# A two-layer encoder on one core: feed-forward x at another address, a memset on another engine, sums one slot later, scale rows by transposes

## The chip, the core and the metric

The kernel runs on 1 core of one Trainium2 chip. The metric is the device time of one execution in microseconds. The engines go by these names: PE is TensorE (matrix products), PEld its weight load, DVE VectorE, ACT ScalarE, POOL GpSimd, SP SyncE. ACTq and SPq are the queues from which ACT and SP issue DMAs. Each engine works through its own queue in the order in which the program emitted its instructions; semaphores hold an instruction until what it reads or overwrites is ready.

## What is computed

An encoder of two layers over 256 tokens of width 2048, in 32-bit floating point. Each layer adds a mixer (an mLSTM, a retention and an attention with low-rank projections) and a feed-forward part to x:

```python
for l in range(DEPTH):                                  # DEPTH = 2
    h = _rms(x, g_mix[l])
    x = x + _mixer(h, cos, sin, w_in[l], ...)           # h @ w_in, three groups of heads, y @ w_out
    u = _rms(x, g_ffn[l])
    x = x + jnp.square(jax.nn.relu(u @ w_ff1[l])) @ w_ff2[l]   # 2048 -> 8192 -> 2048
return _rms(x, g_final)
```

`_rms` divides each token by its root mean square and multiplies each column by a gain. The kernel applies the gain when it transposes x, and the division by the token (`rs`, one number for each token) only to the products.

## The kernel before

**Operands.** Every large product is done with its operands split into a high and a low part (float32r, names ending in hi and lo): of the four partial products three are computed. x itself (`xx`, two tiles of 128 tokens) stays in SBUF. Its transposed, scaled and split copy is `xT`: for each of 16 blocks of 128 columns (index k) 256 tokens high and then 256 tokens low, so 512 numbers or 2 KB for each partition and k. `make_xT` (L516) writes it anew before each mixer and each feed-forward part, a quarter (b = 0 to 3) at a time: TensorE transposes, ACT writes the high part, DVE the low one. It starts at byte 37632 of each partition, a multiple of 256.

**The weights** are streamed through the chip once. `Stream` (L230) lets SP fetch chunks of 128 x 1024 (512 KB, `wraw`, four buffers); for each chunk ACT makes `whi` (L308) and DVE `wlo` (L309), four buffers each, prepared up to three chunks ahead of PE. Three kinds of loops use them:

- `nat` and `nat_steps` (L464 to L486): x or y is the stationary operand and 512 columns of weights move past it; three matmuls for each k and token tile.
- `stat` (L488): a 128 x 128 piece of weights is stationary and the 256 tokens move.
- `ff_tile` (L1170), the first product of the feed-forward part (FF1): the piece of `whi` is stationary while high and low x move together, 512 wide, and then the piece of `wlo` while high x moves, 256 wide. The sum is tile `f`. There are 64 tiles f for each layer with 16 such pairs each, 2048 pairs in all.

**The feed-forward part** runs in groups of 8 tiles f. While FF1 works at group gi + 1, the second product (FF2) is done for group gi, half of it by plain `nat_steps` into the tiles `pk`, and half by the seven products of a Strassen scheme (`product`, L1194; tiles `pa`, `pd`, `pe`). So the loop at L1251 has slots i = 0 to 7: FF1 of one tile f, product i (not in the last slot), one chunk of plain FF2. The Strassen scheme needs sums of weights (`su`, `sb`, on DVE, L286 to L292) and sums of activations (`ff_sums`, L1152): for each half of a group four DVE instructions into `fsum`, two on ACT (`shi`) and two on DVE (`slo`). The first half's sums of group gi + 1 are handed out after slot i = 4, six times in each layer.

**The order of the work.** Side work (transposes, evacuations, softmax, sums) is written as generators. `pump` (L451) is called between the matmuls with the time that they are thought to take, and lets at most two side tasks that are due make one step. So the order on every queue is fixed when the program is written out, by the estimates given to `yield` and `pump`; a step more or less in one task shifts its neighbours.

**The mLSTM values.** `ev_mlv` (L848) gets a buffer `mlv` of 4 heads x 2 token tiles x 129 columns, sets the last column of each to one (L852, DVE, 128 x 8), and lets ACT copy the values from PSUM beside it (L854), which has to wait for that memset. Ahead of the memset in DVE's queue are the mLSTM convolutions (L834 to L837).

**The token scale.** `token_scale` (L531) reduces the sums of squares, takes the root (`rsqrt`) and then needs `rs`, which lies across partitions, as a row that is repeated in all partitions. For the feed-forward part it does so with two TensorE transposes and a DVE copy (tile `rsf`). For the mixer, at the start of each layer, it writes `rs` to memory (`rs_rows`, L548) and reads it back into all partitions (`rsb`, L550): two DMAs from ACT's queue. `rsb` is first read at L824.

Of the kernel before, what the change touches and what calls it, by code (L numbers as in the profile page):

```python
# [10 lines left out]
F32 = mybir.dt.float32  # L11
F32R = mybir.dt.float32r
# [6 lines left out]
P = 128  # L19
S = 256  # L20
D = 2048
DEPTH = 2
KT = D // P
# [19 lines left out]
G_MIX, G_FFN, G_ML, G_RET, G_Q, G_KV, W_CONV, B_GATE, PAR_W = 0, 16, 32, 36, 40, 44, 46, 70, 86  # L43
# [277 lines left out]
def encoder_kernel(ctx: ExitStack, tc: tile.TileContext, xin, posin, w, par, const, gfin, out, dump=None):  # L321
    nc = tc.nc
    plan = weight_plan()
    one = ctx.enter_context(tc.tile_pool(name="one", bufs=1))
    wp = ctx.enter_context(tc.tile_pool(name="wp", bufs=4))
    ap = ctx.enter_context(tc.tile_pool(name="ap", bufs=1))
    sp = ctx.enter_context(tc.tile_pool(name="sp", bufs=2))
    pm = ctx.enter_context(tc.tile_pool(name="pm", bufs=4, space=PSUM))
    pside = ctx.enter_context(tc.tile_pool(name="pside", bufs=4, space=PSUM))
    dp = ctx.enter_context(tc.tile_pool(name="dp", bufs=2, space=bass.MemoryType.DRAM))  # L330
    ctx.enter_context(tc.manual_schedule())

    V, A, T = nc.vector, nc.scalar, nc.tensor
# [2 lines left out]

    cst = one.tile([P, C_W], F32, name="cst")
    head = one.tile([P, P + DEPTH * PAR_W], F32, name="head")
    pos = one.tile([P, 2], I32, name="pos")
    ss = one.tile([P, 2, 4], F32, name="ss")  # L340
    rs = one.tile([P, 2], F32, name="rs")

    one.tile([P, 40], F32, name="pad")
    xx = one.tile([P, 2, D], F32, name="xx")
    x = [xx[:, t, :] for t in range(2)]
    xT = one.tile([P, KT, 2, S], F32R, name="xT")
    cosf = one.tile([P, 2, 64], F32, name="cosf")
    sinf = one.tile([P, 2, 64], F32, name="sinf")

# [6 lines left out]
    for i, cw in enumerate((256, 256, 512, 512, 512)):  # L356
        nc.sync.dma_start(out=xx[:, :, c0:c0 + cw],
                          in_=xin[:, c0:c0 + cw].rearrange("(t p) c -> p t c", p=P))
# [14 lines left out]
    def bank(name):  # L373
        return pside.tile([P, 512], F32, name=name, tag="s")

    def sumsq(src, acc, width):
        junk = sp.tile([P, 512], mybir.dt.bfloat16, name="junk", tag="junk", bufs=1)
        A.activation(junk[:, :width], src, AF.Square, accum_out=acc)
# [15 lines left out]
    def split(*items):  # L394

        for hi, lo, src, *g in items:
            A.activation(hi, src, AF.Copy, **({"scale": g[0]} if g else {}))
        for hi, lo, src, *g in items:
            if g:
                V.scalar_tensor_tensor(lo, src, g[0], hi.bitcast(F32), op0=ALU.mult, op1=ALU.subtract)  # L400
            else:
                V.tensor_tensor(lo, src, hi.bitcast(F32), op=ALU.subtract)  # L402

    def tr(dst, src, n=P):
        T.transpose(dst, src, ident[:n, :n])
# [8 lines left out]
    class Task:  # L414
# [24 lines left out]
        def finish(self, n=1 << 30):  # L439
            for d in self.after:  # L440
                d, m = d if isinstance(d, tuple) else (d, 1 << 30)
                d.finish(m)
            while not self.done and self.n < n:
                self.step()

    def add(gen, after=(), delay=0.0):
        t = Task(gen, list(after), delay)
        side.append(t)
        return t
# [53 lines left out]
    xt_task = {}  # L503

    def xboth(k):
        if k // 4 in xt_task:
            xt_task[k // 4].finish(1 + k % 4 // 2)
        return xT[:, k, :, :]

    def xh(k):  # L510
        return xboth(k)[:, 0, :]
# [3 lines left out]

    def make_xT(b, g0, l, wait):  # L516

        for pr in range(2):
            ps = bank("xt")
            for j in range(2):  # L520
                k = 4 * b + 2 * pr + j
                for t in range(2):
                    tr(ps[:, j * S + t * P:j * S + (t + 1) * P], x[t][:, k * P:(k + 1) * P])
            k = 4 * b + 2 * pr
            split(*[(xT[:, k + j, 0, :], xT[:, k + j, 1, :], ps[:, j * S:(j + 1) * S],
                     prm[:, l, g0 + k + j:g0 + k + j + 1]) for j in range(2)])
            yield 0.8 if pr == 0 else wait
        for t in range(2):
            sumsq(x[t][:, b * 512:(b + 1) * 512], ss[:, t, b:b + 1], 512)

    def token_scale(rows_by_pe):  # L531
        tot = sp.tile([P, 2], F32, name="tot", tag="tot")
        V.tensor_reduce(tot, ss, axis=AX.X, op=ALU.add)
        yield from rsqrt(rs, tot, 2, 1.0 / D)
        if rows_by_pe:
            yield 1.0
            rsb = sp.tile([P, 2, P], F32, name="rsf", tag="rsb", bufs=1)
            ps = bank("rsf")
            for t in range(2):
                tr(ps[:, t * P:(t + 1) * P], rs[:, t:t + 1].broadcast_to([P, P]))  # L540
            V.tensor_copy(hflat(rsb), ps[:, :S])
            scale_rows.append(rsb)
            return
        rows = dp.tile([2, P], F32, name="rs_rows")
        rsb = sp.tile([P, 2, P], F32, name="rsb", tag="rsb", bufs=1)
        scale_rows.append(rsb)
        yield 2.4
        nc.scalar.dma_start(out=rows.rearrange("t p -> p t"), in_=rs)  # L548
        yield 8.0
        nc.scalar.dma_start(out=rsb, in_=rows.unsqueeze(0).broadcast_to([P, 2, P]))  # L550

    def new_xT(b, g0, l, rows_by_pe, wait=0.8):

        xt_task[b] = add(make_xT(b, g0, l, wait), [(xt_task[b - 1], 2)] if b else [])
        if b == 3:
            xt_last[:] = [add(token_scale(rows_by_pe), xt_task.values(), 1.2)]

    xt_last = []
    scale_rows = []
# [55 lines left out]
    def hflat(tl):  # L615
        return tl.rearrange("p a b -> p (a b)")

    def layer(l):
        g = prm[:, l, :]
        L = {}  # L620


        def ev_cq(ps):
            L["cq"] = ap.tile([P, 2, 512], F32, name="cq", tag="nat", bufs=2)
            L["sq"] = sp.tile([P, 2, 2], F32, name="sq", tag="sq", bufs=1)
            for t in range(2):
                A.activation(L["cq"][:, t, :], ps[t], AF.Copy, scale=rs[:, t:t + 1])
                sumsq(L["cq"][:, t, :], L["sq"][:, 0, t:t + 1], 512)

        def cq_task():  # L630
            cq = L["cq"]
            L["chi"] = ap.tile([P, 6, S], F32R, name="chi", tag="hhi", bufs=2)
            L["clo"] = ap.tile([P, 6, S], F32R, name="clo", tag="hlo", bufs=2)
# [214 lines left out]
        def ev_mlv(ps):  # L848
            finish(gat)
            v = ap.tile([P, 1088], F32, name="mlv", tag="mlv")[:, :1032].rearrange("p (a b c) -> p a b c", a=2, b=4)  # L850
            L["mlv"] = v
            V.memset(v[:, :, :, 128:129].rearrange("p a b c -> p (a b c)"), 1.0)  # L852
            for t in range(2):
                A.activation(v[:, t, :, 0:128], ps[t].rearrange("p (h c) -> p h c", h=4), AF.Copy,  # L854
                             scale=rs[:, t:t + 1])
# [182 lines left out]
        for h in range(0, 8, 4):  # L1038
            ps = [pm.tile([P, 512], F32, name="pm", tag="m") for _ in range(2)]
# [9 lines left out]
        for h in range(0, 8, 2):  # L1049
            ps = pm.tile([P, 512], F32, name="pm", tag="m")  # L1050
# [16 lines left out]
        for i in range(2):  # L1067
            chunks = take()
            pss = []
            for pr in range(2):  # L1070
                ps = pm.tile([P, 512], F32, name="pm", tag="m")
# [43 lines left out]
        for b in range(2):  # L1115
            nat_steps(take(), pss[b], yh, yl, 0, False, True)
            ev_x(b)(pss[b])
            new_xT(b, G_FFN, l, True)
        for b in range(2, 4):
            nat(take(), yh, yl, ev_x(b))  # L1120
            new_xT(b, G_FFN, l, True)


        hts, qs, fs, evs = {}, {}, {}, {}

        def ff_evac(f, ps):
# [111 lines left out]
        ps = [bank("f") for i in range(2)]  # L1238
# [12 lines left out]
        for gi in range(NGRP - 1):  # L1251
            more = gi + 1 < NGRP - 1
            for i in range(8):
                ff1((gi + 1) * 8 + i)
                if i < 7:
                    product(gi, i)
                if not keep:
                    keep += [[pm.tile([P, 512], F32, name="pk", tag="m") for _ in range(2)] for _ in range(2)]
                nat_steps(take(), keep[i // 4], hk(gi, 0), hk(gi, 1), 0, gi == 0 and i % 4 == 0,
                          i == 7 and not more and l == DEPTH - 1)  # L1260
                if more and i == 4:
                    sums[gi + 1, 0] = add(ff_sums(gi + 1, 0), [evs[(gi + 1) * 8 + 3]])
            if more:
                sums[gi + 1, 1] = add(ff_sums(gi + 1, 1), [evs[(gi + 1) * 8 + 7], sums[gi + 1, 0]])
# [4 lines left out]
        for b in range(4):  # L1269
            if l == DEPTH - 1 and b == 3:  # L1270
                last_block(take(), lh, ll)
                return
            ps = keep[b - 2] if b >= 2 else [bank("pb") for t in range(2)]
            nat_steps(take(), ps, lh, ll, 0, b < 2, True)
            ev_x(b)(ps)
            if l + 1 < DEPTH:
                new_xT(b, G_MIX, l + 1, False)
            else:
                add(final_part(b))

# [64 lines left out]
                nc.sync.dma_start(out=out[tok, b * 512:(b + 1) * 512], in_=xs)  # L1345

    for b in range(4):
        new_xT(b, G_MIX, 0, False, 5.0)
    ws.prep(1)
    xt_task[0].finish(1)  # L1350
    tables = [add(rope_tables(), [xt_task[3]])]
# [31 lines left out]
```

## Time and profile before

| | us |
|---|---|
| median of 3 runs | 2151.51 (2151.40 to 2151.62) |
| the profiled execution's own time | 2152.16 |
| its span in the trace | 2150.3 |

The granted clock of TensorE over that execution was 0.997. A row of the profile's list of groups names line, engine and operation, what is written and read, and the count, then busy time, mean duration in ns, and the idle time of the engine ahead of these instructions with what ended it. In a stretch of the timeline a row has start, duration, engine, line, operation, and in brackets the idle time before it. Matmuls overlap: the next one starts while the one before still drains, so the cost of a matmul is read from one start to the next and not from the duration shown.

### The profile page before, as it was taken

The page shows a single profiled execution, that of the slowest core. Times are in us where ns is not written, and L with a number is a line of the kernel's source. Part 1 is how long each engine was busy: PE and PEld are TensorE (multiplying, and loading weights), DVE is VectorE, ACT ScalarE, POOL GpSimd, SP SyncE. Part 2 cuts the span into 40 slices and gives each one's busy share as a digit, 9 for nine tenths or more (in the row PEclk, how much of TensorE's full clock was granted, in tenths as well). Part 3 has the DMA queues.
Part 4 walks back from the last instruction along what each step waited for, and adds up shares of the span by engine and source line. Part 5 has one row for each costly group of instructions (what it writes and reads, how often), then busy time and mean ns, then how long its engine had stood idle before and what let it go on. Part 6 is the DMA issues. An engine that isn't in the chain of part 4 may idle for free.

```text
span 2150.3 us, 29544 instructions
## 1 busy us (share of the span) xinstructions
PE 2121.0 (99%) x11116; PEld 1811.4 (84%) x11116; DVE 1607.2 (75%) x2371; ACT 1215.0 (57%) x1802; POOL 4.1 (0%) x7
## 2 busy tenths in 40 slices
PE   8999999999999999999999999999999999999998
PEld 7898888888888888888888978888888888888887
DVE  5767575788878888887666675758878888788875
ACT  6645655555655555555556456556555555565554
POOL 0000000000000000000000000000000000000000
PEclk9999999999999999999999999999999999999999
DMA  7544555656566566575575454557566565665664
GB/s 212 186 147 134 170 177 186 199 172 227 162 210 208 165 210 201 166 233 160 181 187 173 131 162 133 184 179 234 156 214 196 169 231 156 212 203 168 211 190 158
DMA packets 111359, 395.22 MB, mean 184 GB/s; under 512 B 12904, under 2 KB 14056, under 8 KB 111088
## 3 DMA queue, kind: packets, MB, share of 16 engines
q1 hardware_dynamic: 109072, 389.90, 56.7%
q10 hardware_dynamic: 2144, 3.43, 0.5%
q8 instruction: 87, 1.43, 0.3%
q14 instruction: 56, 0.46, 0.1%
HBM read 391.17 MB, written 2.12 MB: 183 GB/s over the span
## 4 chain that ended last, share of the span: by engine, by line
PE 80%; DVE 12%; ACT 3%; issue 3%; DMA 1%; ACTq 0%; SPq 0%; DVEq 0%
PE f L408 27%; PE pm L408 26%; PE pk L408 13%; DVE wlo L309 6%; ACT whi L308 2%; PE pb L408 2%; PE pa L1221 2%; PE pa L1223 2%; PE pa L1222 2%; DVE sb L290 1%; DMA wraw<-in_w_dram 1%; DVE su L292 1%; PE sc L408 1%; DVE slo L402 1%; DVE xx L1230 1%
## 5 line engine op out<-in xcount | busy, mean ns | idle before, releaser
L309 DVE TENSOR_TENSOR wlo<-wraw,whi 128x1024 fp32r<-128x1024 f32 (+2 forms) x681 | 825.7, 1216 | 286.8 <-ACT whi L308 284.8
L308 ACT ACTIVATE whi<-wraw 128x1024 fp32r<-128x1024 f32 (+2 forms) x681 | 704.8, 1051 | 207.2 <-PE f L408 86.5
L408 PE MATMUL f<-xT,whi 128*128 128x512 f32 x2048 | 731.9, 398 | 0.0
L408 PE MATMUL f<-xT,wlo 128*128 128x256 f32 x2048 | 554.2, 281 | 0.0
L408 PEld LDWEIGHTS f<-xT,whi 128*128 128x128 f32 x2048 | 384.1, 188 | 86.5
L408 PEld LDWEIGHTS f<-xT,wlo 128*128 128x128 f32 x2048 | 386.5, 189 | 11.6
L408 PE MATMUL pm<-whi,xT 128*128 128x512 f32 (+1 forms) x896 | 289.9, 392 | 6.7 <-ACT whi L308 5.0
L408 PE MATMUL pk<-wlo,hhi 128*128 128x512 f32 x496 | 194.4, 392 | 6.2 <-DVE wlo L309 6.2
L408 PEld LDWEIGHTS pm<-whi,xT 128*128 128x128 f32 x896 | 168.5, 191 | 37.8 <-ACT whi L308 6.1
L408 PE MATMUL pk<-whi,hhi 128*128 128x512 f32 x496 | 193.5, 390 | 0.0
L408 PE MATMUL pk<-whi,hlo 128*128 128x512 f32 x496 | 193.2, 389 | 0.0
L408 PE MATMUL pm<-wlo,xT 128*128 128x512 f32 (+1 forms) x448 | 172.4, 385 | 3.6 <-DVE wlo L309 3.6
L1138 ACT ACTIVATE fr<-f 128x256 f32<-128x256 f32 x128 | 48.2, 376 | 152.5 <-PE f L408 152.5
L308 ACT ACTIVATE whi<-su 128x1024 fp32r<-128x1024 f32 x84 | 87.3, 1054 | 72.1 <-DVE su L288 68.3
L309 DVE TENSOR_TENSOR wlo<-su,whi 128x1024 fp32r<-128x1024 f32 x84 | 100.3, 1219 | 34.1 <-ACT whi L308 34.1
L408 PEld LDWEIGHTS pk<-wlo,hhi 128*128 128x128 f32 x496 | 93.1, 188 | 30.3 <-DVE wlo L309 11.3
L1145 ACT ACTIVATE fq<-fu 128x256 f32<-128x256 f32 x128 | 53.6, 418 | 104.2 <-DVE fu L1143 104.1
L408 PEld LDWEIGHTS pk<-whi,hlo 128*128 128x128 f32 x496 | 93.1, 188 | 19.1
L408 PEld LDWEIGHTS pk<-whi,hhi 128*128 128x128 f32 x496 | 93.1, 188 | 18.8
L1139 DVE TENSOR_TENSOR fr<-f,fr 128x256 f32<-128x256 f32 x128 | 53.8, 421 | 65.2 <-ACT fr L1138 65.1
L408 PEld LDWEIGHTS pm<-wlo,xT 128*128 128x128 f32 x448 | 85.6, 191 | 19.4 <-DVE wlo L309 5.9
L408 PE MATMUL pm<-whi,yhi 128*128 128x512 f32 x256 | 101.5, 397 | 0.0
(295 smaller groups left out, 3066.4 us busy)
## 6 DMA issues: line engine op xcount, KB each, us to landing
wraw<-in_w_dram SPq DMA_DIRECT2D x667, 512.0 KB, 3.8
sb<-in_w_dram SPq DMA_DIRECT2D x56, 512.0 KB, 5.9
wraw<-in_w_dram SPq DMA_DIRECT2D x10, 504.0 KB, 6.9
wt<-mx_rows ACTq DMA_DIRECT2D x8, 256.0 KB, 3.5
out_dram<-xx SPq DMA_DIRECT2D x8, 256.0 KB, 3.1
xx<-in_x_dram SPq DMA_DIRECT2D x3, 512.0 KB, 7.7
gf<-in_gfin_dram ACTq DMA_DIRECT2D x1, 1024.0 KB, 5.5
xx<-in_x_dram SPq DMA_DIRECT2D x2, 256.0 KB, 4.2
```

Source lines behind the costliest of these rows:

```text
L290: V.tensor_tensor(held["b12"][:, h, :], held["b12"][:, h, :], held["b22"][:, h, :], op=ALU.add)
L292: V.tensor_tensor(held["u"][:, h, :], held["u"][:, h, :], last, op=ALU.add)
L308: self.nc.scalar.activation(hi[:, :f], raw, AF.Copy)
L309: self.nc.vector.tensor_tensor(lo[:, :f], raw, hi[:, :f].bitcast(F32), op=ALU.subtract)
L402: V.tensor_tensor(lo, src, hi.bitcast(F32), op=ALU.subtract)
L408: T.matmul(ps, lhsT=lhsT, rhs=rhs, start=start, stop=stop)
L1138: A.activation(r, ps[:, S:], AF.Copy)
L1139: V.tensor_tensor(r, ps[:, :S], r, op=ALU.add)
L1145: A.activation(q, u, AF.Square)
L1221: T.matmul(ps, lhsT=ha, rhs=wh, start=st, stop=False, skip_group_check=True)
L1222: T.matmul(ps, lhsT=ha, rhs=wl, start=False, stop=False, skip_group_check=True)
L1223: T.matmul(ps, lhsT=la, rhs=wh, start=False, stop=kp == 3, skip_group_check=True)
```

## The change

Four edits, made together:

1. **x of the feed-forward part lies 32 bytes on.** `xT` becomes a buffer that is 16 numbers longer, with two views of the same shape: one at offset 0, which the mixer uses, and one at offset 8 numbers (32 bytes), which the feed-forward part uses, for writing and for reading. `xx` and the buffer are allocated ahead of `pos`, `ss` and `rs`, and the pad shrinks from 40 to 24 numbers, so that the mixer's view starts at byte 37376 (again a multiple of 256), the feed-forward's at 37408, and everything from `cosf` on stays at its address.
2. **The ones of `mlv`** are set by GpSimd in place of DVE.
3. **The first half of the sums** of the next group is handed out after slot 5 and not after slot 4.
4. **The mixer's token scale rows** are made as the feed-forward's always were, by two transposes and a DVE copy; the two DMAs through memory go. The tile is named `rsb` in both places.

```diff
-    one.tile([P, 40], F32, name="pad")
-    xx = one.tile([P, 2, D], F32, name="xx")
-    xT = one.tile([P, KT, 2, S], F32R, name="xT")
+    xx = one.tile([P, 2, D], F32, name="xx")
...
+    xbuf = one.tile([P, KT * 2 * S + 16], F32R, name="xT")
+    views = [xbuf[:, o:o + KT * 2 * S].rearrange("p (k a s) -> p k a s", k=KT, a=2) for o in (0, 8)]
+    view = [0]
...
+    one.tile([P, 24], F32, name="pad")
...
     def xboth(k):
...
-        return xT[:, k, :, :]
+        return views[view[0]][:, k, :, :]
...
     def make_xT(b, g0, l, wait):
+        xT = views[1 if g0 == G_FFN else 0]
...
-    def token_scale(rows_by_pe):
+    def token_scale():
         tot = sp.tile([P, 2], F32, name="tot", tag="tot")
         V.tensor_reduce(tot, ss, axis=AX.X, op=ALU.add)
         yield from rsqrt(rs, tot, 2, 1.0 / D)
-        if rows_by_pe:
...
-        rows = dp.tile([2, P], F32, name="rs_rows")
+        yield 1.0
         rsb = sp.tile([P, 2, P], F32, name="rsb", tag="rsb", bufs=1)
+        ps = bank("rsb")
+        for t in range(2):
+            tr(ps[:, t * P:(t + 1) * P], rs[:, t:t + 1].broadcast_to([P, P]))
+        V.tensor_copy(hflat(rsb), ps[:, :S])
         scale_rows.append(rsb)
-        yield 2.4
-        nc.scalar.dma_start(out=rows.rearrange("t p -> p t"), in_=rs)
-        yield 8.0
-        nc.scalar.dma_start(out=rsb, in_=rows.unsqueeze(0).broadcast_to([P, 2, P]))
...
-            V.memset(v[:, :, :, 128:129].rearrange("p a b c -> p (a b c)"), 1.0)
+            nc.gpsimd.memset(v[:, :, :, 128:129].rearrange("p a b c -> p (a b c)"), 1.0)
...
+        view[0] = 1
...
-                if more and i == 4:
+                if more and i == 5:
                     sums[gi + 1, 0] = add(ff_sums(gi + 1, 0), [evs[(gi + 1) * 8 + 3]])
```

Three places of the order show what moves. The first is DVE's queue in the feed-forward part of layer 0, where the first half of a group's sums stands (`fsum`, `slo`; `wlo` are the low parts of chunks of weights, `su` the sum of weights for the Strassen scheme, `fr` a step of the evacuation of a tile f; a number behind a name counts the buffers). Before:

```order
L292 TENSOR_TENSOR su<-su,wraw_5192 128x1024
L309 TENSOR_TENSOR wlo_5307<-wraw_5192,whi_5306 128x1024
L1160 TENSOR_TENSOR fsum<-fq 128x256
L1161 SCALAR_TENSOR_TENSOR fsum<-fq,fsum 128x256
L1163 SCALAR_TENSOR_TENSOR fsum<-fsum,fq 128x256
L1164 TENSOR_TENSOR fsum<-fq 128x256
L292 TENSOR_TENSOR su<-su,wraw_5256 128x1024
L309 TENSOR_TENSOR wlo_5339<-wraw_5256,whi_5338 128x1024
L402 TENSOR_TENSOR slo_5321<-fsum,shi_5320 128x2x256
L402 TENSOR_TENSOR slo_5323<-fsum,shi_5322 128x2x256
L309 TENSOR_TENSOR wlo_5366<-wraw_5273,whi_5365 128x1024
L1139 TENSOR_TENSOR fr<-f,fr 128x256
```

The same sums in the queue of after, where they stand behind other chunks:

```order
L309 TENSOR_TENSOR wlo_5406<-su,whi_5405 128x1024
L1157 TENSOR_TENSOR fsum<-fq 128x256
L1158 SCALAR_TENSOR_TENSOR fsum<-fq,fsum 128x256
L1160 SCALAR_TENSOR_TENSOR fsum<-fsum,fq 128x256
L1161 TENSOR_TENSOR fsum<-fq 128x256
L309 TENSOR_TENSOR wlo_5435<-su,whi_5434 128x1024
L404 TENSOR_TENSOR slo_5418<-fsum,shi_5417 128x2x256
L404 TENSOR_TENSOR slo_5420<-fsum,shi_5419 128x2x256
L309 TENSOR_TENSOR wlo_5459<-wraw_5334,whi_5458 128x1024
L1136 TENSOR_TENSOR fr<-f,fr 128x256
L309 TENSOR_TENSOR wlo_5475<-wraw_5357,whi_5474 128x1024
```

The six instructions move from between the two `su` sums of product 5 to between the two chunks of product 6 (`wlo<-su`), which need no new sum of weights. The two `shi` on ACT move with them.

The second place is ACT's queue in layer 0, behind the first chunks of the mixer (`chi` is the split latent of the attention, `g_eu` and `g_r` are the mLSTM's gates, `krh` the rotary key, and an ACT_TABLE_LOAD fetches the table of another function). Before:

```order
L308 ACTIVATE whi_707<-wraw_590 128x1024
L397 ACTIVATE chi<-ckvt,head 128x256 x2
L308 ACTIVATE whi_735<-wraw_617 128x1024
L762 ACT_TABLE_LOAD
L762 ACTIVATE g_eu<-g_eu 4x512
L308 ACTIVATE whi_771<-wraw_652 128x1024
L767 ACT_TABLE_LOAD
L767 ACTIVATE g_r<-g_eu 4x512
L681 ACTIVATE krh<-krt 128x256
L308 ACTIVATE whi_798<-wraw_678 128x1024
```

And after:

```order
L308 ACTIVATE whi_708<-wraw_591 128x1024
L399 ACTIVATE chi<-ckvt,head 128x256 x2
L758 ACT_TABLE_LOAD
L758 ACTIVATE g_eu<-g_eu 4x512
L308 ACTIVATE whi_737<-wraw_618 128x1024
L763 ACT_TABLE_LOAD
L763 ACTIVATE g_r<-g_eu 4x512
L308 ACTIVATE whi_774<-wraw_653 128x1024
L677 ACTIVATE krh<-krt 128x256
L308 ACTIVATE whi_803<-wraw_679 128x1024
```

The token scale task of layer 0 has fewer steps, so the tasks behind it come due elsewhere: `krh` and the gates have changed places with chunks of weights. From the evacuation of c_q on to the mLSTM's columns, layer 0's order on PE, ACT and DVE is now the one that layer 1 has, before and after alike.

The third is GpSimd's queue behind its start. Before:

```order
L1379 UNCONDITIONAL_BRANCH
L363 MEMSET krl 128x256
L964 MEMSET rq 128x2048 x2
L1379 UNCONDITIONAL_BRANCH
L1379 ISA
```

After:

```order
L1376 UNCONDITIONAL_BRANCH
L365 MEMSET krl 128x256
L848 MEMSET mlv 128x8
L960 MEMSET rq 128x2048
L848 MEMSET mlv 128x8
L960 MEMSET rq 128x2048
L1376 UNCONDITIONAL_BRANCH
```

Each layer's memset of ones stands ahead of that layer's memset of `rq`, and behind nothing else of its layer.

More of the change, by code (lines that the diff above doesn't have):

```diff
@@ L338, in encoder_kernel @@
     head = one.tile([P, P + DEPTH * PAR_W], F32, name="head")
+    xx = one.tile([P, 2, D], F32, name="xx")
+    x = [xx[:, t, :] for t in range(2)]
+    xbuf = one.tile([P, KT * 2 * S + 16], F32R, name="xT")
+    views = [xbuf[:, o:o + KT * 2 * S].rearrange("p (k a s) -> p k a s", k=KT, a=2) for o in (0, 8)]
+    view = [0]
     pos = one.tile([P, 2], I32, name="pos")
@@ L341, in encoder_kernel @@
     rs = one.tile([P, 2], F32, name="rs")
-    one.tile([P, 40], F32, name="pad")
-    xx = one.tile([P, 2, D], F32, name="xx")
-    x = [xx[:, t, :] for t in range(2)]
-    xT = one.tile([P, KT, 2, S], F32R, name="xT")
+    one.tile([P, 24], F32, name="pad")
     cosf = one.tile([P, 2, 64], F32, name="cosf")
@@ L534, in token_scale, with new_xT @@
         yield from rsqrt(rs, tot, 2, 1.0 / D)
-        if rows_by_pe:
[L536 to L543, printed above, removed]
-        rows = dp.tile([2, P], F32, name="rs_rows")
+        yield 1.0
         rsb = sp.tile([P, 2, P], F32, name="rsb", tag="rsb", bufs=1)
+        ps = bank("rsb")
+        for t in range(2):
+            tr(ps[:, t * P:(t + 1) * P], rs[:, t:t + 1].broadcast_to([P, P]))
+        V.tensor_copy(hflat(rsb), ps[:, :S])
         scale_rows.append(rsb)
-        yield 2.4
-        nc.scalar.dma_start(out=rows.rearrange("t p -> p t"), in_=rs)
-        yield 8.0
-        nc.scalar.dma_start(out=rsb, in_=rows.unsqueeze(0).broadcast_to([P, 2, P]))
-    def new_xT(b, g0, l, rows_by_pe, wait=0.8):
+    def new_xT(b, g0, l, wait=0.8):
         xt_task[b] = add(make_xT(b, g0, l, wait), [(xt_task[b - 1], 2)] if b else [])
         if b == 3:
-            xt_last[:] = [add(token_scale(rows_by_pe), xt_task.values(), 1.2)]
+            xt_last[:] = [add(token_scale(), xt_task.values(), 1.2)]
     xt_last = []
@@ L620, in layer @@
         L = {}
+        view[0] = 0
         def ev_cq(ps):
@@ L1117, in layer @@
             ev_x(b)(pss[b])
-            new_xT(b, G_FFN, l, True)
+            new_xT(b, G_FFN, l)
         for b in range(2, 4):
             nat(take(), yh, yl, ev_x(b))
-            new_xT(b, G_FFN, l, True)
+            new_xT(b, G_FFN, l)
+        view[0] = 1
         hts, qs, fs, evs = {}, {}, {}, {}
@@ L1276, in layer @@
             if l + 1 < DEPTH:
-                new_xT(b, G_MIX, l + 1, False)
+                new_xT(b, G_MIX, l + 1)
             else:
@@ L1347, in encoder_kernel @@
     for b in range(4):
-        new_xT(b, G_MIX, 0, False, 5.0)
+        new_xT(b, G_MIX, 0, 5.0)
     ws.prep(1)
```

## Prediction

> **What bounds the kernel now.** I read the page's engine line first, then the chain, then what TensorE waited for.
>
> ```profile
> PE 2121.0 (99%) x11116; PEld 1811.4 (84%) x11116; DVE 1607.2 (75%) x2371; ACT 1215.0 (57%) x1802; POOL 4.1 (0%) x7
> PE 80%; DVE 12%; ACT 3%; issue 3%; DMA 1%; ACTq 0%; SPq 0%; DVEq 0%
> L408 PE MATMUL f<-xT,whi 128*128 128x512 f32 x2048 | 731.9, 398 | 0.0
> ```
>
> PE is busy in all but 29 of 2150 us and carries 80% of the chain. So time can go in two ways: PE stops less, or a matmul takes less. The waits of PE say how much the first holds (total, times, longest):
>
> ```profile
> PE pk L408 <- DVE wlo L309: 6.2, 12, 0.5
> PE pm L408 <- DVE wlo L309: 5.6, 10, 0.9
> PE pm L408 <- ACT whi L308: 5.0, 3, 2.0
> ...
> PE krt L405 <- DVE kr L676: 0.9, 2, 0.5
> ```
>
> Twelve equal stalls are in the feed-forward part, in `pk`; most of the rest are in the mixers. For the second way one needs the time from start to start, since shown durations overlap. From PE's timeline, x stationary with 512 weights moving (nine matmuls between the first two rows), and then weights stationary with 256 of x moving (six):
>
> ```profile
> 1276.75 0.62 PE L408 MATMUL pm<-whi,xT 128*128 128x512 f32 x2
> ...
> 1278.79 0.39 PE L408 MATMUL pm<-whi,xT 128*128 128x512 f32 x1
> ```
>
> ```profile
> 140.40 0.28 PE L408 MATMUL pm<-xT,wlo 128*128 128x256 f32 x1
> ...
> 141.12 0.28 PE L408 MATMUL pm<-xT,wlo 128*128 128x256 f32 x1
> ```
>
> 2.04 / 9 = 226.7 ns and 0.72 / 6 = 120 ns. An FF1 pair (512 and 256) should therefore take 346.7 ns. Two tiles `f` show what it takes; from the first to the second row there are 13 pairs, from the third to the last 14:
>
> ```profile
> 391.22 0.40 PE L408 MATMUL f<-xT,whi 128*128 128x512 f32 x1
> ...
> 395.73 0.39 PE L408 MATMUL f<-xT,whi 128*128 128x512 f32 x1
> ...
> 578.87 0.39 PE L408 MATMUL f<-xT,whi 128*128 128x512 f32 x1
> ...
> 579.56 0.40 PE L408 MATMUL f<-xT,whi 128*128 128x512 f32 x1
> ...
> 579.92 0.40 PE L408 MATMUL f<-xT,whi 128*128 128x512 f32 x1
> ...
> 583.80 0.40 PE L408 MATMUL f<-xT,whi 128*128 128x512 f32 x1
> ```
>
> 4.51 / 13 = 346.9 in the early tile and 4.93 / 14 = 352.1 in the later one, which is like nearly all others; within it, pairs take up to 0.36. Averaged over the trace, with the ends of tiles, I take 352.8: an excess of 6.1 ns x 2048 = 12.5 us, with no wait shown.
>
> **Part 1: x 32 bytes on.** Removed or added: nothing but an address. The views of 2 KB for each k overlap the mixer's only where the mixer has long finished, so no new wait. The excess is found where 512 numbers of x move, and not where x is stationary (226.7) or moves 256 wide (120). The early tile used the same x addresses and ran without it, so it can go away; it is a matter of how the reads fall, to which the address may belong. No row shows an operand of these matmuls off a multiple of 256 bytes, so the price is bounded by rows: at best the 512 matmul falls to 226.7 while the 256 one stays at its present 117 (pairs of 344), -18 us; nothing; at worst all pairs as the slowest, 0.36, +15 us, and for a matmul disturbed twice see the rival. I take the pair of the early tile, 346.7 to 346.9, as the nearest row: **-12.5 us**.
>
> A rule of the Trainium skill, TensorE: Matmul & The Clock Gate, Step-by-step: what each phase is for, speaks against this term: TensorE has two independent read ports into SBUF, so that loading weights takes no bandwidth from the moving operand; by it no address should matter and the term is 0. The trace agrees with it where x is stationary (226.7 with a load behind every matmul), and leaves it open in FF1.
>
> **Part 2: the sums one slot later.** One of the twelve stalls, on PE and on DVE:
>
> ```profile
> 575.31 0.39 PE L408 MATMUL pk<-whi,hhi 128*128 128x512 f32 x1
> 576.22 0.50 PE L408 MATMUL pk<-wlo,hhi 128*128 128x512 f32 x1 [0.52 <-DVE wlo L309]
> 576.56 0.40 PE L408 MATMUL pk<-whi,hlo 128*128 128x512 f32 x1
> ```
>
> ```profile
> 569.89 0.42 DVE L1160 TENSOR_TENSOR fsum<-fq 128x256 f32<-128x256 f32 x1
> ...
> 571.48 1.22 DVE L292 TENSOR_TENSOR su<-su,wraw 128x1024 f32<-128x1024 f32 x1
> ...
> 573.75 1.28 DVE L402 TENSOR_TENSOR slo<-fsum,shi 128x512 fp32r<-128x512 f32 x2
> 574.95 1.22 DVE L309 TENSOR_TENSOR wlo<-wraw,whi 128x1024 fp32r<-128x1024 f32 x1
> ...
> 582.86 1.23 DVE L309 TENSOR_TENSOR wlo<-wraw,whi 128x1024 fp32r<-128x1024 f32 x1 [0.55 <-ACT whi L308]
> ```
>
> Two matmuls took 576.56 - 575.31 = 1.25 us where 2 x 0.227 = 0.45 are due: 0.80 us, which is the idle 0.52 and 0.28 that don't show as idle; I use the idle plus 0.28 for other stalls. DVE has no gap from 569.89 to past the late `wlo` at 574.95: in that stretch lie the sums (569.89 to 571.48 and 573.75 to 574.95, 2.8 us) and a weight sum of 1.2 us. In the next slot, product 6, there is no weight sum, and DVE waits for ACT again at 582.86, 0.55 us. The sums arrive there with 1.2 us more room for each chunk that needs none, and the `wlo` behind them were ready 2 us and more ahead of PE; 2.8 us in four pieces uses that up but for little. On ACT the two `shi` move with them, and it waits between its chunks there, too. All twelve stalls go: 12 x 0.80 = **-9.6 us**. If the cover is short, the same stalls come back in slot 6, smaller or equal: 0 to -9.6, the nearest row is the gap, so the far end.
>
> **Part 3: the ones of `mlv`.**
>
> ```profile
> 204.74 1.27 ACT L854 ACTIVATE mlv<-pm,rs 128x512 f32<-128x512 f32 x2 [7.56 <-DVE mlv L852]
> ```
>
> ```profile
> 207.00 0.50 PE L408 MATMUL pm<-whi,xT 128*128 128x512 f32 x1 [1.46 <-ACT whi L308]
> 208.26 0.50 PE L408 MATMUL pm<-wlo,xT 128*128 128x512 f32 x1 [0.76 <-DVE wlo L309]
> ...
> 211.74 0.50 PE L408 MATMUL pm<-wlo,xT 128*128 128x512 f32 x1 [0.42 <-DVE wlo L309]
> ...
> 1272.55 1.06 PE L408 MATMUL pm<-whi,xT 128*128 128x512 f32 x2
> ...
> 1275.83 0.40 PE L408 MATMUL pm<-wlo,xT 128*128 128x512 f32 x1
> ```
>
> ACT stands 7.56 us for a memset that is queued on DVE behind the convolutions, the next `whi` stands behind ACT's copy, and PE stops three times: 1.46 + 0.76 + 0.42 + 3 x 0.28 = 3.5 us. Layer 1 has the same first two stalls, and then eight matmuls from 1272.55 to 1275.83 in 3.28 us where 1.8 are due: 1.46 + 0.76 + 0.56 + 1.5 = 4.3 us. GpSimd is idle (4.1 us busy in all), so its memset is done long before and ACT's copy starts as soon as PE has the values. What is late next is `wlo`: DVE stays in the convolutions to 204.6, so its chunk ends about 205.8, about when PE wants it, and the one behind, 1.2 us and a gate product of 0.7 later each, I expect some 0.8 us late. So 0.9 us stays for each layer: -2.6 - 3.4 = **-6.0 us**, bounds -4 (a second stall of full size stays) to -7.8 (none stays).
>
> **Part 4: token scale rows.**
>
> ```profile
> rs_rows<-rs ACTq DMA_DIRECT2D x2, 1.0 KB, 9.9
> ```
>
> ```profile
> 48.19 1.04 ACT L308 ACTIVATE whi<-wraw 128x1008 fp32r<-128x1008 f32 x1 [7.75 <-DMA wraw<-in_w_dram]
> ```
>
> ```profile
> 49.29 0.42 PE L408 MATMUL pm<-whi,xT 128*128 128x336 f32 x1 [2.03 <-ACT whi L308]
> 50.53 0.65 PE L408 MATMUL pm<-wlo,xT 128*128 128x336 f32 x1 [0.82 <-DVE wlo L309]
> ...
> 1145.65 0.39 PE L408 MATMUL pm<-chi,wlo 128*128 128x256 f32 x1 [0.90 <-DVE wlo L309]
> ```
>
> ```profile
> 48.00:60.00 12.00, 9.89 (x46) 8.90 (x47) 8.48 (x23) 8.95 (x17) 0.00 (x0) 0.86 0.69 229
> ```
>
> In layer 0 the write of 1 KB takes 9.9 us, and the chunk of weights issued after it lands so late that ACT stands 7.75 us and PE stops: 2.03 + 0.82 + 0.56 = 3.4 us, and the clock granted over 48 to 60 is 0.86, which I put at 1.5 us more: -4.9. In layer 1 there is no PE stall by it: 0. What is added, as it runs in the feed-forward part:
>
> ```profile
> 390.65 0.38 PE L405 MATMUL rsf<-head,rs 128*128 128x128 f32 x2
> 390.79 0.47 PE L408 MATMUL f<-xT,whi 128*128 128x512 f32 x1
> 391.10 0.28 PE L408 MATMUL f<-xT,wlo 128*128 128x256 f32 x1
> ```
>
> 0.14 us for two transposes and 0.08 in the matmul behind; with a short wait for `rs` 0.45 each time, +0.9; the DVE copy (0.4 us) hides beside matmuls. Third, layer 0's order behind it becomes layer 1's, which has stalls where layer 0 has none: 0.9 for `kr` and 0.90 at 1145.65, with 3 x 0.28 and a smaller one 3.1 us: +3.1. Together **-0.9 us**, bounds -4 (no ripple) to +1.
>
> **The sum**, against the profiled execution: 2152.16 - 12.5 - 9.6 - 6.0 - 0.9 = 2123.2; that execution lies 0.65 above the median, so **2122.6 us**.
>
> **The rivals.**
>
> - *The address changes nothing.* PE reads x as before, and pairs stay at 352. For it: no wait is shown, and the early tile shows that the same addresses can run either way. Against it: only the wide x shows the excess. 2122.6 + 12.5 = 2135.1 us; 30%. Halfway (the excess stays in half of the pairs) 2128.9; 10%.
> - *The sums meet a full DVE in slot 6 as well.* The gap of 0.55 at 582.86 is shorter than 2.8 us of sums. All twelve stalls stay: 2122.6 + 9.6 = 2132.2 us; 9%.
> - *Slower: the shifted read costs.* PE may read x more slowly from the new address, in each FF1 matmul. It decides from the pair's time: the other parts give -16.5, so from 352.8 + 16.5 / 2.048 = 360.9 ns on the kernel is slower. The row for a disturbed matmul is the slow pair's 0.36, 13.3 ns over 346.7; that once for each matmul gives 373.3 ns, +42 - 16.5 = +25.5: 2177 us. Against it: no such loss is seen anywhere. 7% at that size, 4% between (about 2150).
>
> **How the numbers follow.** Full relief has 40%, so it sets the predicted time; its own range is 2114 to 2128 (parts 3 and 4 at their ends, 18 in place of 12.5). The range of all, 2114 to 2143: from there to the case without relief at 2135 with parts 2 to 4 each some way short (+8). Left out: the slower rivals (11%) and some 6% at the ends. A measurement of this kernel can tell about 0.2%, 4.3 us, from no change, so faster means under 2147.2 and slower over 2155.8: faster 87%, same 5%, slower 8%.
>
> **What would show it.** Right: 14 pairs of a tile in 4.85 us and not 4.93; no `pk` row among PE's waits; ACT's copy at L854 without a wait; no wait of ACT for a DMA near 48 us; krt stalls four times and not two. Wrong: pairs at 352 or above 361, `pk` waits twelve times elsewhere, or a `wlo` stall of over 1 us behind `mlv`.

## The result and the profile after

The changed kernel takes 2135.3 us (median of 4 runs, 2134.4 to 2136.5) against 2151.57 for the kernel before: a ratio of 0.9924, interval 0.9907 to 0.9941, so 16.3 us faster. The prediction was 2122.6, with a range of 2114 to 2143. Two of its four terms held, two did not: the new address was worth half of what was put down for it, and the scale rows by transposes cost time.

The page's engine line and chain after, then all that TensorE waited for over 0.6 us except for the start:

```profile
PE 2111.1 (99%) x11120; PEld 1811.4 (85%) x11120; DVE 1607.4 (75%) x2371; ACT 1218.1 (57%) x1802; POOL 4.4 (0%) x9
PE 94%; DVE 3%; ACT 1%; DMA 1%; issue 1%; SPq 0%; ACTq 0%; DVEq 0%
```

```profile
PE pm L410 <- DVE wlo L309: 5.6, 10, 0.9
PE rsb L407 <- DVE rs L394: 3.2, 1, 3.2
PE krt L407 <- DVE kr L672: 1.9, 4, 0.5
PE pm L410 <- ACT xT L399: 1.4, 1, 1.4
```

The row of twelve `pk` waits is gone and so is that of the `pm` waits for ACT's `whi`; DVE's share of the chain falls from 12% to 3%. Two things are new: one wait of 3.2 us at the transposes of the scale rows, and four stalls at `krt` in place of two. PE's busy time fell by 9.9 us, so matmuls got shorter as well.

**The new wait.** PE's timeline in layer 0 around the transposes, and the step of DVE that they wait for:

```profile
31.35 0.40 PE L410 MATMUL pm<-whi,xT 128*128 128x512 f32 x1
34.91 0.41 PE L407 MATMUL rsb<-head,rs 128*128 128x128 f32 x2 [3.16 <-DVE rs L394]
...
35.86 1.05 PE L410 MATMUL pm<-whi,xT 128*128 128x512 f32 x2
...
39.04 0.40 PE L410 MATMUL pm<-wlo,xT 128*128 128x512 f32 x1
```

```profile
34.61 0.16 DVE L394 SCALAR_TENSOR_TENSOR rs<-nt 128x2 f32<-128x2 f32 x1
```

PE stands in its queue at the transposes from 31.6 on, and the step that writes `rs` starts at 34.61. Afterwards eight matmuls, from 35.86 on, take 3.18 us, 0.40 each where 0.227 are due; the granted clock from 35.33 to 38.74 us was 0.50. So the place costs 3.3 us of waiting and about 1.7 more in slow matmuls up to 39.0 (two transposes and ten matmuls in 4.13 us where 2.41 are due): as much as the stall at 49.29 that went with the two DMAs. Further on, layer 0 now has the stalls that only layer 1 had:

```profile
77.80 0.30 PE L407 MATMUL krt<-head,kr 128*128 128x128 f32 x1 [0.53 <-DVE kr L672]
...
85.76 0.38 PE L410 MATMUL pm<-chi,wlo 128*128 128x256 f32 x1 [0.91 <-DVE wlo L309]
```

**The FF1 tiles.** One slot of the feed-forward part before (the start of its FF1 tile at 578.87 stands in the prediction): the first product matmul behind the tile, and the first matmul of the next tile.

```profile
584.52 0.40 PE L1221 MATMUL pa<-whi,hhi 128*128 128x512 f32 x1
...
589.97 0.39 PE L408 MATMUL f<-xT,whi 128*128 128x512 f32 x1
```

The same slot after, from the tile's first matmul:

```profile
577.72 0.40 PE L410 MATMUL f<-xT,whi 128*128 128x512 f32 x1
...
583.29 0.40 PE L1218 MATMUL pa<-whi,hhi 128*128 128x512 f32 x1
...
588.76 0.40 PE L410 MATMUL f<-xT,whi 128*128 128x512 f32 x1
```

The tile (16 pairs) takes 5.57 us and not 5.65. Sixteen pairs at 346.7 would be 5.547. But the 24 matmuls behind it, which don't read x at all, take 5.47 where they took 5.45 (24 x 226.7 = 5.44). Medians over the slots, taken start to start from the trace: 5.647 and 5.447 before, 5.570 and 5.477 after. Over all 128 tiles that is a gain of 9.5 us (77 ns in most, next to nothing in two at the start of each layer), and the stretches of FF2 behind the tiles give 30 ns each back, 3.3 us: 6.2 us are left. The whole of FF1 in one layer, from its first matmul to the first one behind its last tile and with the FF2 in between, says the same: 642.50 us, against 645.58 in the run below that moves the sums alone; neither of the two has a stall there.

**The ones of `mlv`.** ACT's wait at the copy after:

```profile
ACT mlv L850 <- PE pm L410: 4.7, 2, 2.3
```

It waits for PE's values now, 2.3 us each time, and no longer 7.6 for a memset. In layer 0 the stall for `whi` is gone and one `wlo` stall of 0.42 is left:

```profile
213.37 0.50 PE L410 MATMUL pm<-wlo,xT 128*128 128x512 f32 x1 [0.42 <-DVE wlo L309]
```

### The profile page after: what moved, and what is told of

It is laid out like the page before. It is cut to its first block, busy times and chain, and to the rows that moved or that the text cites. A ratio compares the mean times of both kernels' runs of the same rounds, so it can differ in the third digit from the quotient of the medians.

```text
span 2133.5 us, 29557 instructions
## 1 busy us (share of the span) xinstructions
PE 2111.1 (99%) x11120; PEld 1811.4 (85%) x11120; DVE 1607.4 (75%) x2371; ACT 1218.1 (57%) x1802; POOL 4.4 (0%) x9
## 3 DMA queue, kind: packets, MB, share of 16 engines
q10 hardware_dynamic: 1312, 3.16, 0.4%
## 4 chain that ended last, share of the span: by engine, by line
PE 94%; DVE 3%; ACT 1%; DMA 1%; issue 1%; SPq 0%; ACTq 0%; DVEq 0%
PE f L410 33%; PE pm L410 26%; PE pk L410 16%; PE pa L1218 2%; PE pa L1220 2%; PE pa L1219 2%; PE pb L410 2%; PE pd L1218 1%; PE pd L1220 1%; PE pd L1219 1%; DVE wlo L309 1%; PE sc L410 1%; DMA wraw<-in_w_dram 1%; PE pe L1218 1%; PE pe L1220 1%
## 5 line engine op out<-in xcount | busy, mean ns | idle before, releaser
L410 PE MATMUL f<-xT,whi 128*128 128x512 f32 x2048 | 722.8, 392 | 0.0
L410 PE MATMUL pm<-whi,ylo 128*128 128x512 f32 x256 | 99.9, 390 | 0.0
L410 PE MATMUL pm<-wlo,yhi 128*128 128x512 f32 x256 | 99.6, 389 | 0.0
```

What stands on the lines that cost most here:

```text
L410: T.matmul(ps, lhsT=lhsT, rhs=rhs, start=start, stop=stop)
```

## The experiments

Ratios are to the kernel before, measured together with the run; they compare means, and the difference behind a ratio is worked out from it. The medians of the kernel before beside these runs lie between 2151.0 and 2152.2, so times of runs that were not measured together compare to about 1 us.

### Each edit alone

Theory: the four edits act in four places and add up; the fourth one loses. Rival: an edit works through another (pairs that settle differently because the stalls ahead went), or as predicted.

**The address alone** (edit 1 of the diff, put into the kernel before):

```diff
...
-        return xT[:, k, :, :]
+        return views[view[0]][:, k, :, :]
...
```

> The kernel before with only the first edit: x of the feed-forward part 32 bytes on. Theory (the address alone decides how the FF1 pairs settle): pairs go from 352.1 to about 348 ns as in the changed kernel, the twelve stalls of pk and all waits of the mixers stay, and the time falls by 6 to 7 us, to about 2145. Rival one (the pairs changed because the stalls ahead of them went, not because of the address): pairs stay at 352 and the time stays at 2151.5. Rival two (the address is worth the whole excess of 12.5 us and something else in the changed kernel hides half of it): about 2139.

Measured: 2146.8 us, ratio 0.9974 (0.9963 to 0.9984), that is -5.6 us. The same slot in its timeline:

```profile
578.46 0.40 PE L410 MATMUL f<-xT,whi 128*128 128x512 f32 x1
...
584.02 0.40 PE L1227 MATMUL pa<-whi,hhi 128*128 128x512 f32 x1
...
589.50 0.40 PE L410 MATMUL f<-xT,whi 128*128 128x512 f32 x1
```

The tile takes 5.56 to 5.57 and what is behind it 5.48, with all twelve `pk` stalls still there. So the address alone sets it; both rivals fall. The `pk` stalls grew from 6.2 to 7.0 us in all, which is why the time shows less than the 6.2 us of the stretch.

**The sums alone:**

```diff
-                if more and i == 4:
+                if more and i == 5:
```

> The kernel before with only the third edit: the first half of the sums after slot 5. Theory: the twelve pk stalls go and nothing comes in their place, -9.5 us (twelve times 0.80), about 2142; FF1 pairs stay at 352. Rival (the pairs take their time from the stalls ahead of them): pairs go to 348 in this kernel and the time falls by about 16 us, to 2135.5.

Measured: 2141.2 us, ratio 0.9952 (0.9939 to 0.9965), -10.3 us. No `pk` row is left among PE's waits, and FF1 pairs stay at 352.1. The theory holds.

**The ones alone:**

```diff
-            V.memset(v[:, :, :, 128:129].rearrange("p a b c -> p (a b c)"), 1.0)
+            nc.gpsimd.memset(v[:, :, :, 128:129].rearrange("p a b c -> p (a b c)"), 1.0)
```

> The kernel before with only the second edit: the ones of mlv by GpSimd. Theory: ACT's copy waits no more for the memset, the stalls behind it shrink from 3.5 and 4.3 us to about 0.9 each, -6 us in all, about 2145.5. Rival (DVE's low parts are late whatever ACT does): only the stalls for ACT go and those for DVE grow by the same, less than 2 us in all, about 2150.

Measured: 2145.5 us, ratio 0.9970 (0.9958 to 0.9981), -6.5 us, as expected. One `wlo` stall of 0.46 us is left behind the copy in each layer.

**The scale rows alone** (edit 4):

```diff
...
+        for t in range(2):
+            tr(ps[:, t * P:(t + 1) * P], rs[:, t:t + 1].broadcast_to([P, P]))
+        V.tensor_copy(hflat(rsb), ps[:, :S])
         scale_rows.append(rsb)
-        yield 2.4
-        nc.scalar.dma_start(out=rows.rearrange("t p -> p t"), in_=rs)
-        yield 8.0
-        nc.scalar.dma_start(out=rsb, in_=rows.unsqueeze(0).broadcast_to([P, 2, P]))
...
```

> The kernel before with only the fourth edit: the mixer's scale rows by transposes. Theory (the transposes stand in TensorE's queue 3 us ahead of the rs that they need, and the shifted order brings layer 0 the stalls of layer 1): the 4.9 us of the late chunk go, 3.3 us of waiting for rs, 2 us of lower clock and 3.7 us of stalls at kr and chi come: +3 to +5 us, about 2155. Rival (as predicted): the wait for rs is short, -0.9 us, about 2150.6. Rival two (only the wait counts, the order's stalls come from elsewhere): about 2151.

Measured: 2157.5 us, ratio 1.0025 (1.0015 to 1.0035), +5.4 us: slower than the kernel before, with the same wait of 3.17 us at the transposes:

```profile
34.70 0.66 PE L405 MATMUL rsb<-head,rs 128*128 128x128 f32 x2 [3.17 <-DVE rs L392]
```

The four add up: -5.6 - 10.3 - 6.5 + 5.4 = -17.0 us, against -16.3 for the changed kernel; each of these intervals reaches some 2 us either way.

### The address

**16, 48 and 64 bytes** in place of 32, in the changed kernel:

```diff
-    views = [... for o in (0, 8)]
+    views = [... for o in (0, 4)]      # 12 and 16 in the other two
```

> The changed kernel with x of the feed-forward part 16 bytes on instead of 32. Theory (what counts is that x starts off a multiple of 64 bytes): FF1 pairs settle as at 32, 346.6 to 348 ns, time as the changed kernel, about 2135. Rival (32 is special, half of 64): pairs at 352 as before, about 2142. Rival two (each offset sets its own way of settling): pairs at some third value.

> The changed kernel with x of the feed-forward part 48 bytes on. Theory one (the place within 32 bytes counts): as at 16 bytes, about 2130. Theory two (every offset settles in its own way): neither 2130 nor 2135.

> The changed kernel with x of the feed-forward part 64 bytes on instead of 32. Theory (the place within 64 bytes counts): pairs at 352 as before the change, about 2142. Rival (any distance from the old address, and so from the weights' addresses, does it): pairs at 348, about 2135.

| bytes | FF1 tile, us | 24 matmuls behind, us | FF1 of one layer, us | time, us | faster than before by, us |
|---|---|---|---|---|---|
| 0 (the sums alone) | 5.647 | 5.447 | 645.58 | | |
| 16 | 5.552 | 5.442 | 639.49 | 2129.9 | 21.3 |
| 32 (the changed kernel) | 5.570 | 5.477 | 642.50 | 2135.3 | 16.3 |
| 48 | 5.550 | 5.450 | 640.21 | 2130.4 | 21.7 |
| 64 | 5.583 | 5.490 | 644.40 | 2139.4 | 11.6 |
| without any loss | 5.547 | 5.440 | | | |

(Tiles and the matmuls behind them are medians over the slots, from start to start; FF1 of one layer is the stretch described above, and the last column holds all four edits.) The slot with 16 bytes:

```profile
577.56 0.39 PE L410 MATMUL f<-xT,whi 128*128 128x512 f32 x1
...
583.11 0.39 PE L1218 MATMUL pa<-whi,hhi 128*128 128x512 f32 x1
...
588.55 0.39 PE L410 MATMUL f<-xT,whi 128*128 128x512 f32 x1
```

At 16 bytes nearly all of the excess goes: 0.100 us for each slot, and 12.2 us over the two layers by the stretch (2 x 6.09), the 12.5 us of the prediction, of which 32 bytes bring 6.2. At 64 bytes the old state does not return (2.4 us are gained), so the place within 64 bytes is not what counts, and my theory there falls. That of a period of 32 bytes does not fit 32 and 64 against 0. It seems to fit 16 against 48, whose times agree (2129.9 and 2130.4), but the matmuls do not: at 48 bytes the stretch is 0.72 us longer in each layer, and most tiles at the start of a layer, with no FF2 between them, take 5.62 us, where those at 16 take 5.55. Each distance settles in its own way; of the five, the multiples of 32 leave more.

**x stays, and the rest moves.** One view of x, at the multiple of 256 bytes that the mixer's view has, and a pad that is 32 bytes shorter, so that all behind it (weights, activations, sums) lies 32 bytes lower:

```diff
-    views = [... for o in (0, 8)]
+    views = [... for o in (0, 0)]
...
-    one.tile([P, 24], F32, name="pad")
+    one.tile([P, 16], F32, name="pad")
```

> The changed kernel with one view of x, at its old multiple of 256 bytes, and everything behind it (weights, activations, sums) 32 bytes lower. Theory one (what counts is how x lies to the weights): FF1 settles as in the changed kernel, pairs about 348, time about 2135. Theory two (x's own address counts): pairs at 352, and time about 2142. Theory three (any operand off its place disturbs every matmul): slower than 2142.

```profile
579.17 0.40 PE L410 MATMUL f<-xT,whi 128*128 128x512 f32 x1
...
584.74 0.40 PE L1218 MATMUL pa<-whi,hhi 128*128 128x512 f32 x1
...
590.22 0.40 PE L410 MATMUL f<-xT,whi 128*128 128x512 f32 x1
```

5.57 and 5.48, the two sums of the changed kernel, with x at a multiple of 256 bytes as before the change: 2136.8 us. So, for the one distance that was made both ways, the distance from x to what the other matmuls and the weight loads read counts, and not x's own address. The Trainium skill, TensorE: Matmul & The Clock Gate, Step-by-step: what each phase is for, has weight loads and the moving operand on two independent read ports, so that one takes nothing from the other. By that no distance would matter; tiles of 5.647, 5.570 and 5.552 us with the same instructions say that for 512 columns of x at 4 bytes each it does.

**The mixer's x moved as well:**

```diff
-    views = [... for o in (0, 8)]
+    views = [... for o in (8, 8)]
```

> The changed kernel with the mixer's x 32 bytes on as well, so that there is one view. In the mixer x is the stationary operand, or moves 256 wide. Theory (only wide reads of x care): those matmuls keep 226.7 and 120 ns, the time stays at about 2135. Rival (a weight load from the shifted address is slower, or loses against the moving weights): the mixer's matmuls, some 1350 with x stationary, get a few ns each, about 5 us slower, 2140.

Measured: 2135.7 us against 2135.3, no difference that these runs can tell. But the trace has two, which nearly cancel. Between the first two rows lie twelve matmuls with x stationary, between the last two 21 with 256 of x moving, each from start to start:

```profile
1271.84 0.63 PE L410 MATMUL pm<-whi,xT 128*128 128x512 f32 x2
...
1274.64 0.40 PE L410 MATMUL pm<-whi,xT 128*128 128x512 f32 x1
```

```profile
135.60 0.40 PE L410 MATMUL pm<-xT,whi 128*128 128x256 f32 x2
...
138.06 0.39 PE L410 MATMUL pm<-xT,whi 128*128 128x256 f32 x2
```

2.80 / 12 = 233 ns where 226.7 stood in the prediction's rows, and 2.46 / 21 = 117 where 120 stood. Over the whole trace, without idle time, the 1344 matmuls with x stationary take 3.2 us more than in the changed kernel and the 768 with 256 of x moving 2.1 us less. So the theory that only wide reads of x care falls, and the rival was right about the few ns for each matmul with x stationary, though not about the time. Two views save 1.1 us over one by this, less than the times can show. The run above, in which the rest moved, has the same in its mixers: medians of 233 and 117 ns, where the changed kernel has 227 and 120. So there, too, the distance counts.

### The scale rows

**Asked for later.** The changed kernel, with the old steps of 2.4 and 8.0 us ahead of the mixer's transposes (`ffn` is true for the feed-forward part):

```diff
...
-        yield 1.0
+        yield 1.0 if ffn else 2.4
+        if not ffn:
+            yield 8.0
...
```

> The changed kernel with the mixer's scale rows asked for at the time at which the old kernel read them back from memory (steps of 2.4 and 8.0 us ahead of the transposes), so that layer 0 keeps the order that it had before the change. Theory (the fourth edit lost by waiting for rs and by the order that it shifted): no wait at the transposes, no lower clock there, two krt stalls and not four: 9 us less than the changed kernel, about 2126.5. Rival (the stalls of layer 0 come from the missing DMAs letting the weights run ahead, not from the order): only the wait goes, about 2130.

Measured: 2126.5 us, ratio 0.9887 (0.9873 to 0.9900). The transposes in layer 0:

```profile
42.36 0.32 PE L410 MATMUL pm<-whi,xT 128*128 128x336 f32 x1
42.51 0.38 PE L407 MATMUL rsb<-head,rs 128*128 128x128 f32 x2
42.65 0.40 PE L410 MATMUL pm<-whi,xT 128*128 128x336 f32 x1
```

They cost 0.14 us and wait for nothing. Layer 0 has its order back, and PE's windows of 60 to 140 us show it, of the changed kernel and of this one:

```profile
60.00:140.00 80.00, 77.39 (x521) 70.09 (x521) 53.01 (x98) 46.48 (x65) 0.11 (x1) 1.00 0.51 166
```

```profile
60.00:140.00 80.00, 80.00 (x566) 74.70 (x565) 54.67 (x97) 47.23 (x69) 0.11 (x1) 1.00 0.50 168
```

PE is busy for all of 80 us and not for 77.4. So the edit's idea was sound, and its place in the queue lost it.

**Layer 1 in the order of layer 0.** A delay of 3.9 in place of 3.0 for layer 1's c_q task gives layer 1 the order that layer 0 has in the run above, on DVE and PE:

```diff
-        cqt = add(cq_task(), delay=3.0)
+        cqt = add(cq_task(), delay=3.0 if l == 0 else 3.9)
```

> The run with late scale rows, and layer 1's c_q task due 0.9 us later, so that layer 1's order on DVE and TensorE behind it becomes the one of layer 0. Theory (the stalls at kr and chi go with the order, whichever layer has it): they vanish in layer 1 as well, 3 to 3.5 us less than with late rows alone, about 2123. Rival (they belong to layer 1, whose weights arrive in another rhythm): no change, 2126.5.

Measured: 2122.8 us, ratio 0.9864 (0.9851 to 0.9878), 3.6 us less than with late rows alone. The two were not measured together and differ by 5.0 by their ratios; layer 1's four stalls there, 2.44 us and 0.28 for each, make 3.6. PE's waits have no `krt` row any more, and seven waits for `wlo` in place of ten in the changed kernel:

```profile
PE pm L410 <- DVE wlo L309: 3.0, 7, 0.8
...
PE pm L410 <- ACT xT L399: 1.0, 1, 1.0
```

The stalls belong to the order, whichever layer has it.

**All of it, with 16 bytes:**

```diff
-    views = [... for o in (0, 8)]
+    views = [... for o in (0, 4)]
```

> The same with x of the feed-forward part at 16 bytes instead of 32. Theory (the gain of 5.4 us between the offsets is a matter of the FF1 pairs and of the products right behind them, and does not depend on the mixers): 5.4 us less, about 2117.5. Rival (the way in which the pairs settle hangs on the timing ahead of the feed-forward part): pairs other than with 16 bytes before, anything from 2117 to 2125.

Measured: 2117.3 us (2117.0 to 2117.4), ratio 0.9838 (0.9825 to 0.9852): 35 us faster than the kernel before and 18 faster than the changed one. The run before it, with 32 bytes, was measured together with this one: the 5.4 us between 32 and 16 bytes come out again as 5.6.

## Why the prediction was right or wrong

- **Part 2, the sums (-9.6):** right in place, mechanism and size. Alone -10.3; the cover in slot 6 held, and no `wlo` was late there.
- **Part 3, the ones (-6.0):** right. Alone -6.5, with one `wlo` stall of 0.46 us left in each layer, 0.74 with the 0.28 that doesn't show as idle, where 0.9 were put down.
- **Part 1, the address (-12.5):** the mechanism was right (pairs lose time by where x lies, not by a wait), the size was not. The step that failed took the early tile's pair, 346.7 to 346.9, as what every pair would come to. At 32 bytes the pairs do come near that, 348 over 14 of them, but only from the fourth one on; and the sum had no term for the matmuls behind the tile, which pay 30 ns a slot. Measured: -5.6 alone, -6.2 by the stretch of FF1. Full relief was there to be had at 16 bytes. The rival "halfway" (2128.9) came nearest to the size of this term. The premise that only wide reads of x show an excess was too narrow: with the mixer's x moved, its other matmuls changed too, and in the trace of before some three in ten of the matmuls with x stationary take 231 ns or more; the 226.7 came from nine of the others.
- **Part 4, the scale rows (-0.9):** wrong, with the wrong sign: +5.4. The step "with a short wait for `rs` 0.45 each time" failed. It took for granted that PE reaches the transposes when `rs` is ready. In the queue they stand behind the sixth matmul of a chunk. The trace of before had both times, that matmul (the first of the two in the row) and the last step of `rs`:

```profile
30.89 0.62 PE L408 MATMUL pm<-whi,xT 128*128 128x512 f32 x2
```

```profile
34.16 0.16 DVE L392 SCALAR_TENSOR_TENSOR rs<-nt 128x2 f32<-128x2 f32 x1
```

  PE is there at 31.1 and `rs` comes at 34.2, 3 us later; the two were not set beside each other. The rest of the part was right: the late chunk's stall went, and the ripple of layer 0's order came at +3.7 where 3.1 stood.
- **The sum:** both misses go the same way, 6.3 us in part 1 (by the stretch) and 6.3 in part 4. So the time fell on the 2135.1 of the rival in which the address changes nothing, for another reason: the address did change something, and the fourth edit took as much away. The time alone would have confirmed the wrong case; the pairs at 348 and the wait at `rsb` are what tells them apart. That the range held is luck to this extent: its slow end was drawn for an address that changes nothing and parts 2 to 4 somewhat short, and it happened to cover a half relief and a part with the wrong sign.
- **What was to be seen:** 14 pairs in 4.85 us (4.87), no `pk` row, no wait of ACT for a DMA near 48 us, four `krt` stalls: these came. ACT's copy without a wait did not: it waits 2.3 us each time for PE, and only the wait for the memset is gone. The page's new row of 3.2 us was not on the list.

Open: what it is in the reads that makes a pair's time hang on that distance, and why the disturbance lasts for some matmuls that don't read x. The runs show only that it does, and that of the distances tried 16 bytes leave next to none.

## What to carry to other kernels

When an operation moves into the queue of the engine that bounds the kernel, set two times beside each other before counting it as hidden: when that engine gets to the place, and when its operand is written; a cheap instruction at the wrong place cost more here than the slow transfer it replaced. Where matmuls take more from start to start than others of their shape, with no wait shown, try a few distances between the operands, not one, and measure the matmuls behind as well. Equal times do not say that nothing changed: two effects of opposite sign can hide in them, as with the mixer's x. Several edits in one change should each be run alone: the sum here hid a loss of 5 us.

## What the runs showed of the hardware

With the same instructions, a tile of 16 pairs takes 5.55 to 5.65 us by the distance between x and the rest of SBUF, at the five distances from 0 to 64 bytes that were tried. At 32 bytes between them (the run with the mixer's x moved) matmuls with x stationary go from 227 to 234 ns in median, and those with 256 of x moving from 120 to 117. And the disturbance outlasts the tile; the first matmuls behind it, in the changed kernel:

```profile
583.29 0.40 PE L1218 MATMUL pa<-whi,hhi 128*128 128x512 f32 x1
...
584.91 0.39 PE L1219 MATMUL pa<-wlo,hhi 128*128 128x512 f32 x1
```

Seven matmuls in 1.62 us, 231 ns each, of which none reads x; after them the spacing is back at 227.

A stop of 3.16 us, with one of 0.75 us some 4 us ahead of it, was followed by a granted clock of 0.50 from 35.33 to 38.74 us; over 30 to 42 us it was 0.86, and 1.00 in the run with late rows, which has no such stop. Shorter stops can do the same, but need not: in the kernel before, stops of 1.46 and 0.76 us in layer 1 were followed by 0.54 over 1272.5 to 1275.9 us, and the same two stops in layer 0 left it at 1.00 over 203 to 215.
